# First MLP step interleaved by column block, memory keys and second block's scores later, last norm's vectors loaded after the output weights

## The chip, the cores and the metric

The kernel runs on one core of a Trainium2 chip. The metric is the device time of one execution in microseconds; a kernel's figure is the median of several runs. The engines are PE (TensorE, the matrix products; PEld are its weight loads), ACT (ScalarE), DVE (VectorE), POOL (GpSimd) and SP (SyncE, which here issues almost all transfers). PSUM holds the results of products in banks, SBUF everything else.

## What is computed

The input is x of 256 positions by 1024 channels, with 256 memory rows. Two hybrid layers and one closing block follow, all in float32:

```
hybrid_layer (twice):
    h = rms_norm(x, ln_mix);  z = h @ w_in
    o_nsa, o_gla, o_mem = sparse attention, gated linear attention, cross-attention into mem
    merged = sum over b of sigmoid(gate_b) * (o_b @ w_branch[b])
    x = x + merged @ w_out
    x = x + square(relu(rms_norm(x, ln_mlp) @ w_up)) @ w_down
second block (once):
    z = x @ w_in;  a gated-MLP branch, a convolution branch, a MoBA attention branch (8 heads)
    merged as above, each branch gated
    x = layer_norm(2 ** 0.25 * x + merged @ w_out, ln_g, ln_b)
```

The keys and values of the cross-attention are rms_norm(mem, mem_norm) @ w_kv, with weights of their own in each layer.

## The kernel before

**Products in three parts.** A float32 weight is loaded raw as 128 x 1024 (512 KB, four buffers `raw`, issued by SP, line 457). `split` (lines 435 to 442) makes its high part on ACT (L441), for every sixth weight on POOL (L439), and its low part raw − high on DVE (L442); `hi` and `lo` have four buffers each. Activations are kept as high and low parts as well (`hilo`, lines 526 to 532: the high part on ACT, L531, the low part on DVE, L532). A product is then high times high, high times low and low times high (`mm3`). In the first MLP matrix the high and low activations stand side by side (tile `hx`), so that one product of 512 columns does two of the three parts and one of 256 columns, with the weight's low part, does the third.

**Order of the work.** The order of PE's instructions is written out by hand: the big products are the trunk, and side work is put in between as *chains*, Python generators that emit some instructions and yield a delay. `pump()` (line 138), called in the trunk after one or a few products, emits what is due by a clock that adds up the estimated durations of the products; `need(hh, k)` (line 157) emits chains until the columns k of an activation exist, and `finish(c)` (line 148) empties a chain. The queues of ACT, DVE, POOL and SP are put in order by a planner: by when an instruction could run in its estimate, and in program order among those that could. PSUM has four accumulators (`acc`), three buffers for side work (`psm`) and one more (`pso`).

**First MLP step.** At the end of the attention part of a layer, `out_proj` (line 1176) adds merged @ w_out to X in two halves of the columns; a chain (`start_x`, `x_transposed`, lines 534 to 559) turns X into the columns `hx`, two column blocks per group of four transposes (L192) into one psm buffer. `up_first` (lines 1364 to 1375) computes the first 512 of the 4096 hidden units. It fills four accumulators: for each half of the contraction (`hf`, four blocks k) and each half of the units (`c`), the code takes column block `cb`, in it first the four products with high weights, then the four with low weights, 64 products in all. X's blocks 4 to 7 are transposed while the first half runs. In layer 0 the memory columns for layer 1's keys are also made here: `mem_start(1, mem1[0], 1000.0)` (line 1401, defined at 604) starts a chain of four groups of four transposes of `gate` (where the memory rows were loaded), due 1000 ns after the step's start and 300 ns after each other. Their conversions write two `b8x` tiles. After the step, `mem_kv` (lines 609 and 1404) multiplies them with the key weights. The relu and square of the step's result follow in `up` (line 1328).

**Second block's attention.** `moba` (lines 1520 to 1579) is one chain over four pairs of heads. `scores(pr)` emits eight score products and four bias products into two psm buffers; DVE takes the maxima, ACT the exponentials (L1542), DVE normalizes. The next pair's scores come 3000 ns later, the transposes of the pair (L1550) 6500 ns after that. Meanwhile the trunk multiplies with w_in. The chain is collected at `finish(c_att)` (line 1616).

**Last projection and norm.** In the second block `out_proj` is called with "none": the first half of the columns as usual, the second half (lines 1178 to 1194) from four more weights, with the layer norm (`fin`, lines 1647 to 1670) following each half of the rows. The norm's gain and offset, each spread over 128 partitions (512 KB), are loaded into the buffer `hx`, which has one copy and is free after the last product with `hx`; the loads (L1641, L1642) stand in the program ahead of the output weights, and they are read at L1666 and L1669.

Of the kernel before, what the change touches and what calls it, by code (L numbers as in the profile page):

```python
# [10 lines left out]
F32 = mybir.dt.float32  # L11
# [8 lines left out]
P = 128  # L20
# [78 lines left out]
def block_kernel(ctx, tc, x_in, mem_in, positions, ln_mix, w_in, b_merge, nsa_q_norm, nsa_k_norm,  # L99
# [5 lines left out]
    nc = tc.nc  # L105
# [7 lines left out]
    big = ctx.enter_context(tc.tile_pool(name="big", bufs=1))  # L113
# [24 lines left out]
    def pump():  # L138
        for c in list(chains):
            while not c[2] and c[1] <= clock[0]:  # L140
                advance(c)
# [15 lines left out]
    def need(hh, k):  # L157
        r = ready.get(id(hh))
        while r is not None and r[1][0] <= k:
            nxt = min(chains, key=lambda d: d[1])  # L160
            if nxt[1] > clock[0]:
                clock[0] = nxt[1]
            advance(nxt)
# [78 lines left out]
    def wrap(ap, dims):  # L242
        return bass.AP(tensor=ap.tensor, offset=ap.offset, ap=dims)
# [218 lines left out]
    def units(w2d, r0, nk, cols, paired=None, fine=False):  # L462
        n = sum(c1 - c0 for c0, c1 in cols)
        per = max(1, 1024 // n)
        if paired:
            c0, c1 = cols[0]
            res = []
            for k in range(0, 4, per):
                srcs = [(slice(64 * j, 64 * j + 64), 0, n,
                         w2d[256 * j + 64 * k:256 * j + 64 * (k + per), c0:c1].rearrange("(a d) n -> d a n", d=64))  # L470
                        for j in range(2)]
                h, lo = unit(srcs, per, n)
                res += [(h[:, j, :], lo[:, j, :]) for j in range(per)]
            return res
        res = []
        k = 0
        while k < nk:
            a = min(per, nk - k)
            rs = w2d[r0 + k * P:r0 + (k + a) * P, :]
            srcs = []  # L480
            o = 0
            for c0, c1 in cols:
                srcs.append((slice(0, P), o, o + c1 - c0, rs[:, c0:c1].rearrange("(a p) n -> p a n", p=P)))
                o += c1 - c0
            h, lo = unit(srcs, a, n, fine and k == 0)
            if fine and k == per:
                fine()
            for j in range(a):
                res.append((h[:, j, :], lo[:, j, :]))
            k += a  # L490
        return res
# [112 lines left out]
    def mem_start(l, MEM, lat=0.0):  # L604
        mh, ml = B8("b8x", FR), B8("b8x", FR)
        start_x(MEM, mh, ml, 32 + 8 * l, None, lat)
        return mh, ml
# [568 lines left out]
    def out_proj(w2d, mg, fin, gcol, mid=None):  # L1176
        for h in range(2):
            if gcol == "none" and h == 1:
                ws = units(w2d, 0, 8, [(512, 1024)])
                ts_ = slice(0, P)  # L1180
                ps = ACC()
                for k, (wh, wl) in enumerate(ws):
                    mm3(ps, mg[0][:, k, ts_], mg[1][:, k, ts_], wh, wl, k == 0, k == 7)
                fin(0, 2, ps)
                fin(0, 4, None)
                ts_ = slice(P, 2 * P)
                for q in range(2):
                    qs = slice(256 * q, 256 * q + 256)
                    ps = ACC()
                    for k, (wh, wl) in enumerate(ws):  # L1190
                        mm3(ps[:, 0:256], mg[0][:, k, ts_], mg[1][:, k, ts_], wh[:, qs], wl[:, qs], k == 0, k == 7)
                    fin(1, 2 + q, ps[:, 0:256])
                fin(1, 4, None)
                continue
            ps = tok_major(mg[0], mg[1], w2d, 0, 8, [(512 * h, 512 * h + 512)])
            for tt in range(2):
                fin(tt, h, ps[tt])
            if gcol == "none":
                continue
            if h == 0:  # L1200
                halves = [1]
                hT = HX()
                hc = start_x(X, *hT, gcol, halves, 1500.0)
                if mid is not None:
                    mid()
        if gcol == "none":
            return None
        halves[0] = 2
        return hT[0], hT[1], hc

    def layer(l, hT):
        hh, hl, hc = hT
# [83 lines left out]
        mg = None  # L1296
        for b in (2, 1, 0):
# [7 lines left out]
            else:  # L1305
                oT = o_nsa
                finish(c_nsa)
                mg = (B8("b8x", FR), B8("b8x", FR))
# [11 lines left out]
        mem1 = []  # L1320
# [43 lines left out]
        def up_first():  # L1364
            p2 = [ACC() for _ in range(4)]
            for hf in range(2):
                for c in range(2):
                    ws = units(w_up[l], 512 * hf, 4, [(256 * c, 256 * c + 256)])
                    for cb in range(2):
                        for part in range(2):  # L1370
                            for k in range(4 * hf, 4 * hf + 4):
                                need(hh, k)
                                up_product(p2[2 * c + cb], k, cb, ws[k - 4 * hf][part], part)
                                pump()
            return p2

        def dn(gi):
# [20 lines left out]
                    pump()  # L1398

        if l == 0:  # L1400
            mhl = mem_start(1, mem1[0], 1000.0)
        up(0)
        if l == 0:
            mem_kv(1, *mhl)
# [12 lines left out]
    def layer_2(hT):  # L1417
# [102 lines left out]
        def moba():  # L1520
            UE = {}

            def scores(pr):
                p = [PS(), PS()]
                for q0, k1 in ((0, P), (P, 256)):
                    for j in range(2):
                        rr = slice(64 * j, 64 * j + 64)
                        mm(p[j][:, q0:q0 + k1], CQ[rr, pr, q0:q0 + P], CK_[rr, pr, 0:k1], q0 == 0, False)
                for j in range(2):
                    sl = SLP[:, 2 * pr + j, :]  # L1530
                    mm(p[j][:, 0:P], sl, DM[:, 0:P], False, True)
                    mm(p[j][:, P:384], sl, DM[:, P:384], False, True)
                res = []
                for j in range(2):
                    n = SM([P, 2], "n0")
                    dve.tensor_reduce(n[:, 0:1], p[j][:, 0:P], op=OP.max, axis=AX, negate=True)
                    dve.tensor_reduce(n[:, 1:2], p[j][:, P:384], op=OP.max, axis=AX, negate=True)
                    e = T2("pexp")[:, 0:384]
                    s = SM([P, 2], "s0")
                    cuts = (slice(0, P), slice(P, 384))  # L1540
                    for i, cs in enumerate(cuts):
                        act(e[:, cs], p[j][:, cs], AF.Exp, bias=n[:, i:i + 1], accum_out=s[:, i:i + 1])  # L1542
                    r = SM([P, 2], "r0")
                    dve.reciprocal(r, s)
                    for i, cs in enumerate(cuts):
                        dve.tensor_scalar(e[:, cs], e[:, cs], r[:, i:i + 1], None, op0=OP.mult)
                    res.append(e)
                UE[pr] = res

            def transp(e):  # L1550
                pt = PS()
                for i in range(3):
                    tr(pt[:, i * P:i * P + P], e[:, i * P:i * P + P], IDF)
                pts = T2("pts")[:, 0:384]
                act(pts, pt[:, 0:384], AF.Copy)
                return pts

            scores(0)
            po = None
            for pr in range(4):  # L1560
                a = pr % 2
                if pr + 1 < 4:
                    yield 3000.0
                    scores(pr + 1)
                yield 6500.0
                t = [transp(e) for e in UE.pop(pr)]
                yield 2000.0
                if a == 0:
                    yield from take_po()
                    po = PO()  # L1570
                for kt in range(2):
                    for j in range(2):
                        h = 2 * pr + j
                        o = po[64 * j:64 * j + 64, 256 * a + P * kt:256 * a + 256]
                        mm(o, CVv[kt][:, h * 64:h * 64 + 64], t[j][:, 256 * kt:256 + P * kt], kt == 0, kt == 1)
                if a == 1:
                    act(AT[:, pr - 1:pr + 1], v2(po), AF.Copy)
                    free_po()
            yield 1000.0
# [56 lines left out]
            oT = (ya, yb, yc)[b] if bi == 2 else (ya, None, yc)[b]  # L1636
            M = merge_branch(w_branch_2[0, b], oT, g, M, bi == 2, mg)

        LGT = big.tile([P, 2, 1024], F32, tag="hx", name="LGT", bufs=1)
        LG = LGT  # L1640
        nc.sync.dma_start(LGT[:, 0], wrap(ln_g_2[0], [[0, P], [1, 1024]]))  # L1641
        nc.sync.dma_start(LGT[:, 1], wrap(ln_b_2[0], [[0, P], [1, 1024]]))  # L1642

        alpha = 2.0 ** 0.25
        fst = {}
# [1 line left out]
        def fin(tt, h, ps):  # L1647
# [20 lines left out]
            for q, qs in enumerate(cuts):  # L1668
                dve.scalar_tensor_tensor(X[:, tt, qs], X[:, tt, qs], rs, LG[:, 1, qs], op0=OP.mult, op1=OP.add)  # L1669
                nc.sync.dma_start(out[0, tt * P:(tt + 1) * P, qs], X[:, tt, qs])  # L1670
        out_proj(w_out_2[0], mg, fin, "none")

    hh0, hl0 = HX()
    hT = [hh0, hl0]
# [43 lines left out]
```

## Time and profile before

| | us |
|---|---|
| runs | 1221.73, 1219.28, 1221.53 |
| median | 1221.53 |
| profiled execution | 1223.66 |
| its span | 1221.9 |
| TensorE busy | 1201.4 (98%) |
| VectorE busy | 871.5 (71%) |
| ScalarE busy | 605.1 (50%) |
| GpSimd busy | 199.5 (16%) |

The profile comes from one execution of the program. The span is the time from its first to its last instruction. The mean granted clock of TensorE is 0.994 of full speed. An instruction's row gives its start, its duration and, in brackets, how long the engine stood idle before it and what released it. Rows of the same kind in a sequence are merged, with their count (x4). Matmuls overlap each other, so the distance from one start to the next, not the duration shown, tells what a product costs.

### The profile page before, as it was taken

The numbers are of one execution on the slowest core, as the hardware profiler recorded it, in microseconds if no ns is written. First come the engines' busy times: TensorE is split into PE (matmuls) and PEld (weight loads), VectorE is DVE, ScalarE is ACT, GpSimd is POOL, SyncE is SP. The second block draws the span as 40 slices with busy tenths as digits, with TensorE's granted clock in tenths as the row PEclk, the third lists the DMA queues.
The fourth block names the chain that finished last, engine by engine and source line by source line (L and its number), as shares of the span: only waits on it lengthen the run. The fifth ranks groups of instructions, "written<-read, shape, count | busy, mean of one in ns | idle before, by whom it ended". The sixth has DMA issues, their size and how long they took to land. (4 is left out here: it accounts for less than half of the span.)

```text
span 1221.9 us, 17759 instructions
## 1 busy us (share of the span) xinstructions
PE 1201.4 (98%) x6553; PEld 1004.8 (82%) x6553; DVE 871.5 (71%) x1457; ACT 605.1 (50%) x988; POOL 199.5 (16%) x235
## 2 busy tenths in 40 slices
PE   9999999999999999999999999999999999999997
PEld 6897777888788888888777888888888997998876
DVE  5977978677665656658868867665555799985677
ACT  7557544434645445466645444554554334443351
POOL 2310220120111112200312020121111111000201
PEclk9999999999999999999989999999999999999999
DMA  8567523676566666657613576656666555466662
GB/s 279 178 178 205 157 88 108 191 220 209 156 186 187 193 193 188 181 158 186 202 59 104 171 200 194 187 176 201 183 197 196 180 174 172 132 184 198 176 206 70
DMA packets 138699, 213.91 MB, mean 175 GB/s; under 512 B 12145, under 2 KB 76757, under 8 KB 138612
## 3 DMA queue, kind: packets, MB, share of 16 engines
q1 hardware_dynamic: 137284, 209.19, 57.8%
q0 software_dynamic: 1152, 3.31, 0.9%
q8 instruction: 51, 0.84, 0.3%
q14 instruction: 36, 0.29, 0.1%
q10 hardware_dynamic: 176, 0.27, 0.1%
HBM read 211.86 MB, written 1.05 MB: 174 GB/s over the span
## 5 line engine op out<-in xcount | busy, mean ns | idle before, releaser
L442 DVE TENSOR_TENSOR lo<-raw,hi 128x1024 fp32r<-128x1024 f32 (+1 forms) x369 | 458.6, 1246 | 219.9 <-ACT hi L441 169.4
L441 ACT ACTIVATE hi<-raw 128x1024 fp32r<-128x1024 f32 (+1 forms) x308 | 322.8, 1057 | 344.4 <-PE acc L188 284.5
L188 PE MATMUL acc<-hi,hx 128*128 128x512 f32 (+1 forms) x1024 | 338.3, 395 | 0.0
L188 PEld LDWEIGHTS acc<-hi,hx 128*128 128x128 f32 x1024 | 192.0, 189 | 40.2 <-issue 4.0
L188 PE MATMUL acc<-lo,hx 128*128 128x512 f32 (+1 forms) x512 | 197.3, 385 | 0.0
L439 POOL TENSOR_SCALAR hi<-raw 128x1024 fp32r<-128x1024 f32 x61 | 74.5, 1222 | 611.4 <-PE acc L188 438.5
L188 PE MATMUL acc<-hi,oh 128*128 128x512 f32 x400 | 157.9, 395 | 0.0
L188 PE MATMUL acc<-lo,oh 128*128 128x512 f32 x400 | 155.9, 390 | 0.0
L188 PE MATMUL acc<-hi,ol 128*128 128x512 f32 x400 | 155.8, 390 | 0.0
L188 PE MATMUL acc<-hx,hi 128*128 128x256 f32 (+1 forms) x704 | 137.7, 297 | 1.7 <-DVE hx L532 1.7
L188 PEld LDWEIGHTS acc<-hx,hi 128*128 128x128 f32 x704 | 110.9, 191 | 6.4 <-issue 2.3
L188 PE MATMUL psm<-hx,hi 128*128 128x512 f32 x448 | 111.8, 391 | 0.0
L188 PEld LDWEIGHTS acc<-lo,hx 128*128 128x128 f32 x512 | 96.9, 189 | 16.4
L188 PE MATMUL acc<-hi,b8x 128*128 128x512 f32 (+1 forms) x336 | 106.1, 388 | 1.4 <-ACT b8x L531 0.8
L188 PE MATMUL acc<-hx,lo 128*128 128x256 f32 x384 | 101.7, 284 | 0.3 <-DVE lo L442 0.3
L188 PEld LDWEIGHTS psm<-hx,hi 128*128 128x128 f32 x448 | 81.4, 189 | 15.1
L188 PEld LDWEIGHTS acc<-hi,ol 128*128 128x128 f32 x400 | 75.1, 188 | 15.9
L188 PEld LDWEIGHTS acc<-hi,oh 128*128 128x128 f32 x400 | 75.2, 188 | 14.7
L188 PEld LDWEIGHTS acc<-lo,oh 128*128 128x128 f32 x400 | 75.2, 188 | 14.6
L188 PEld LDWEIGHTS acc<-hi,b8x 128*128 128x128 f32 x336 | 62.3, 189 | 14.3 <-DVE b8x L532 1.5
L188 PEld LDWEIGHTS acc<-hx,lo 128*128 128x128 f32 x384 | 71.1, 191 | 1.5 <-DVE lo L442 0.5
L1351 POOL TENSOR_TENSOR tmp<-gtmp 128x512 f32<-128x512 f32 x32 | 39.1, 1223 | 165.7 <-ACT gtmp L1346 165.7
(359 smaller groups left out, 1464.4 us busy)
## 6 DMA issues: line engine op xcount, KB each, us to landing
raw<-in_w_in SPq DMA_DIRECT2D x160, 512.0 KB
raw<-in_w_up SPq DMA_DIRECT2D x64, 512.0 KB
raw<-in_w_down SPq DMA_DIRECT2D x64, 512.0 KB
raw<-in_w_branch SPq DMA_DIRECT2D x28, 512.0 KB
raw<-in_w_out SPq DMA_DIRECT2D x24, 512.0 KB
raw<-in_cmp_w SPq DMA_DIRECT2D x32, 256.0 KB
raw<-in_mem_w_kv SPq DMA_DIRECT2D x15, 512.0 KB
raw<-in_w_branch SPq DMA_DIRECT2D x16, 256.0 KB
```

The source lines that it names most:

```text
L188: nc.tensor.matmul(o, l, r, start=start, stop=stop, skip_group_check=True)
L439: pool.tensor_scalar(hi, raw, 1.0, 1.0, op0=OP.mult, op1=OP.mult)
L441: act(hi, raw, AF.Copy)
L442: dve.tensor_tensor(lo, raw, f32(hi), op=OP.subtract)
L1351: pool.tensor_tensor(u, r, r, op=OP.mult)
```

## The change

It has three parts. In `up_first`, for every block k the products of both column blocks are issued one after the other, first all of the high weights, then all of the low ones, and chains are emitted after each two products. The start of the memory chain goes from 1000 to 7000 ns. In `moba`, the scores of pair 1 come 6500 ns after those of pair 0 instead of 3000; the other pairs keep 3000. The loads of the last norm's vectors become a function that `out_proj` calls after it has asked for the weights of the second column half, through its parameter `mid`.

```diff
--- before.py
+++ after.py
@@ -1177,6 +1177,7 @@
         for h in range(2):
             if gcol == "none" and h == 1:
                 ws = units(w2d, 0, 8, [(512, 1024)])
+                mid()
                 ts_ = slice(0, P)
                 ps = ACC()
                 for k, (wh, wl) in enumerate(ws):
@@ -1366,12 +1367,12 @@
             for hf in range(2):
                 for c in range(2):
                     ws = units(w_up[l], 512 * hf, 4, [(256 * c, 256 * c + 256)])
-                    for cb in range(2):
-                        for part in range(2):
-                            for k in range(4 * hf, 4 * hf + 4):
-                                need(hh, k)
+                    for part in range(2):
+                        for k in range(4 * hf, 4 * hf + 4):
+                            need(hh, k)
+                            for cb in range(2):
                                 up_product(p2[2 * c + cb], k, cb, ws[k - 4 * hf][part], part)
-                                pump()
+                            pump()
             return p2
 
         def dn(gi):
@@ -1398,7 +1399,7 @@
                     pump()
 
         if l == 0:
-            mhl = mem_start(1, mem1[0], 1000.0)
+            mhl = mem_start(1, mem1[0], 7000.0)
         up(0)
         if l == 0:
             mem_kv(1, *mhl)
@@ -1560,7 +1561,7 @@
             for pr in range(4):
                 a = pr % 2
                 if pr + 1 < 4:
-                    yield 3000.0
+                    yield 6500.0 if pr == 0 else 3000.0
                     scores(pr + 1)
                 yield 6500.0
                 t = [transp(e) for e in UE.pop(pr)]
@@ -1636,10 +1637,11 @@
             oT = (ya, yb, yc)[b] if bi == 2 else (ya, None, yc)[b]
             M = merge_branch(w_branch_2[0, b], oT, g, M, bi == 2, mg)
 
-        LGT = big.tile([P, 2, 1024], F32, tag="hx", name="LGT", bufs=1)
-        LG = LGT
-        nc.sync.dma_start(LGT[:, 0], wrap(ln_g_2[0], [[0, P], [1, 1024]]))
-        nc.sync.dma_start(LGT[:, 1], wrap(ln_b_2[0], [[0, P], [1, 1024]]))
+        LG = big.tile([P, 2, 1024], F32, tag="hx", name="LG", bufs=1)
+
+        def load_lg():
+            nc.sync.dma_start(LG[:, 0], wrap(ln_g_2[0], [[0, P], [1, 1024]]))
+            nc.sync.dma_start(LG[:, 1], wrap(ln_b_2[0], [[0, P], [1, 1024]]))
 
         alpha = 2.0 ** 0.25
         fst = {}
@@ -1668,7 +1670,7 @@
             for q, qs in enumerate(cuts):
                 dve.scalar_tensor_tensor(X[:, tt, qs], X[:, tt, qs], rs, LG[:, 1, qs], op0=OP.mult, op1=OP.add)
                 nc.sync.dma_start(out[0, tt * P:(tt + 1) * P, qs], X[:, tt, qs])
-        out_proj(w_out_2[0], mg, fin, "none")
+        out_proj(w_out_2[0], mg, fin, "none", load_lg)
 
     hh0, hl0 = HX()
     hT = [hh0, hl0]
```

## Rows read from the trace of the kernel before

**Rows 1.** The page's first section: busy us of each engine, share, instructions

```profile
PE 1201.4 (98%) x6553; PEld 1004.8 (82%) x6553; DVE 871.5 (71%) x1457; ACT 605.1 (50%) x988; POOL 199.5 (16%) x235
```

**Rows 2.** Waits of PE: total us, times, longest us

```profile
PE acc L188 <- DVE hx L532: 1.7, 1, 1.7
...
PE acc L188 <- DVE lo L442: 0.5, 2, 0.3
```

**Rows 3.** Timeline of PE, first MLP step, layer 0: start, us, what, [idle before]

```profile
302.07 1.07 PE L188 MATMUL acc<-hx,hi 128*128 128x512 f32 x4
...
306.29 0.63 PE L192 MATMUL psm<-CF,gate 128*128 128x128 f32 x4 [0.32 <-DVE b8x L532]
306.68 0.36 PE L188 MATMUL acc<-hx,lo 128*128 128x256 f32 x1
...
314.12 0.50 PE L188 MATMUL acc<-hx,hi 128*128 128x512 f32 x1 [1.74 <-DVE hx L532]
...
319.14 0.40 PE L188 MATMUL acc<-hi,b8x 128*128 128x512 f32 x1
```

**Rows 4.** Timeline of PE, first MLP step, layer 1

```profile
776.63 1.07 PE L188 MATMUL acc<-hx,hi 128*128 128x512 f32 x4
...
780.90 0.60 PE L192 MATMUL psm<-CF,X 128*128 128x128 f32 x4
...
783.08 1.09 PE L188 MATMUL acc<-hx,hi 128*128 128x512 f32 x4
...
788.70 0.63 PE L188 MATMUL psm<-hx,hi 128*128 128x512 f32 x2
```

**Rows 5.** Stretches: busy PE, PEld, DVE, ACT, POOL; granted clock, DMA share, GB/s

```profile
302.00:320.00 18.00, 15.60 (x94) 12.95 (x93) 12.00 (x21) 10.26 (x20) 1.55 (x2) 1.00 0.43 125
1060.00:1080.00 20.00, 19.74 (x166) 18.64 (x164) 20.00 (x43) 10.81 (x21) 1.65 (x1) 1.00 0.53 150
```

**Rows 6.** Timeline of all engines, first MLP step, layer 0

```profile
311.36 1.05 POOL L439 TENSOR_SCALAR hi<-raw 128x1024 fp32r<-128x1024 f32 x1 [19.70 <-PE acc L188]
...
312.44 1.23 DVE L442 TENSOR_TENSOR lo<-raw,hi 128x1024 fp32r<-128x1024 f32 x1 [1.02 <-POOL hi L439]
```

**Rows 7.** Timeline of PE, second block's scores, pairs 0 and 1

```profile
1015.69 0.93 PE L188 MATMUL psm<-g,g 64*128 64x128 f32 x8
...
1016.81 0.48 PE L188 MATMUL acc<-hi,hx 128*128 128x512 f32 x1
...
1020.42 0.48 PE L188 MATMUL psm<-g,g 64*128 64x128 f32 x2
1022.07 0.92 PE L188 MATMUL psm<-g,g 64*128 64x128 f32 x6 [1.17 <-ACT pexp L1542]
...
1023.18 0.47 PE L188 MATMUL acc<-hi,hx 128*128 128x512 f32 x1
```

**Rows 8.** Timeline of SP's queue at the output weights

```profile
1175.59 3.49 SPq L457 DMA_DIRECT2D raw<-in_w_out  x2
...
1179.64 0.65 SPq L1642 DMA_DIRECT2D LGT<-in_ln_b  x1
1180.39 16.50 SPq L457 DMA_DIRECT2D raw<-in_w_out  x6
```

**Rows 9.** Chain of waits that ended last: start, us, what

```profile
1180.39 8.11 DMA raw<-in_w_out
```

**Rows 10.** Timeline of all engines at the output projection's start

```profile
1188.61 1.06 ACT L441 ACTIVATE hi<-raw 128x1024 fp32r<-128x1024 f32 x1 [3.53 <-DMA raw<-in_w_out]
...
1190.20 0.49 PE L188 MATMUL acc<-hi,b8x 128*128 128x512 f32 x1 [0.77 <-ACT b8x L531]
...
1191.58 0.73 PE L188 MATMUL acc<-hi,b8x 128*128 128x512 f32 x2 [0.65 <-DVE b8x L532]
```

**Rows 11.** Timeline of all engines where the last norm begins

```profile
1210.95 1.41 DVE L1666 SCALAR_TENSOR_TENSOR X<-X,bmv,LGT 128x512 f32<-128x512 f32 x2
```

**Rows 12.** Timeline of SP's queue in layer 1

```profile
670.76 0.26 SPq L1421 DMA_DIRECT2D a<-in_conv_w  x1
```

## The prediction

> **What bounds the kernel now.** I read the page's first section: TensorE (PE) is busy for 98% of the span; its weight loads overlap that, and no other engine is above 71% [rows 1]. A change that leaves the products as they are can therefore only give back PE's waits, which are 2% of the span, some 20 us, spread over many places. The view of waits by engine and line shows which lie at the edited places; two stand in [rows 2], of 1.7 us and 0.5 us in total. The timeline around each place shows the step that waits, and the table of stretches how full the other engines are there. So I price each part by the PE time lost at its place, then ask what keeps the loss alive.
>
> The profiled execution took 1223.66 us (span 1221.9), 2.13 above the median of the runs, 1221.53. I subtract gains from 1223.66 and take 2.13 off at the end. 0.2% is 2.4 us, about what a measurement of this kernel can tell from no change.
>
> **First MLP step, interleaved, with later memory keys.** In layer 0 the step's 64 products run from 302.07 to 319.14, 17.07 us [rows 3]. The same step of layer 1 runs from 776.63 to 788.70, 12.07 us, without a wait [rows 4]. Layer 0 carries the memory keys besides: four more groups of four transposes. At 0.63 us of one [rows 3] they are 2.52, so 5.00 − 2.52 = 2.5 us are lost. The stretch 302 to 320 says the same: PE is busy 15.60 of 18.00, idle 2.40 [rows 5]. Counting a group by its start-to-start cost (306.29 to 306.68, 0.39, [rows 3]) gives 5.00 − 1.56 = 3.4, my upper bound.
>
> The loss is mostly one wait: 1.74 us at 314.12 for the low part of X's columns [rows 3]. The chain behind it: the memory groups come first (due 1 us after the step begins), fill the three psm buffers and queue their conversions on ACT and DVE; X's last two groups go out only after the fourth of them, at 306.29 [rows 3]. The last group's conversion on DVE then stands behind a weight's low part, started at 312.44 after waiting 1.02 for a POOL split that had begun at 311.36 [rows 6].
>
> After the change the memory groups are due 7 us in. X's last two groups, due some 4 us in by the kernel's clock, come ahead of them, at about 306.6 for the last (an estimate from the due times in the code). Layer 1 gives the spacing without the memory: its last group starts at 780.90 and the second half of the contraction at 783.08 [rows 4], that is 6.45 us after the step's start, so at 308.5 here. Interleaving moves the first use of the last column from the fourth to the seventh product of that half, three products of about 0.23 us later: 308.5 + 1.4 = 309.9, or 3.3 us after its transposes. Layer 1 does it in 2.18 + 0.7 = 2.9. So the 1.74 goes. Of the remaining 0.66 of idle I keep a quarter, since four memory groups still follow one another: taken gain 2.3, bounds 0 (the conversion is still late) and 3.4.
>
> What moves and what follows it: the memory chain issues 16 transposes, their ACT and DVE conversions and no DMA, so SP's queue is passed by nothing and its raw buffers keep their order. POOL keeps its splits and squares. Conversions now lie around 310 to 315, where the stretch has DVE at 12.00 and ACT at 10.26 of 18 [rows 5]. The memory key products follow the step at about 316.8 and need the first columns: about 4 us after their groups, which are at 310 to 312.6. They also need two of the four accumulators; those of column half 0 end 16 products (2.8 us) before the step's end in either order, so the ACT copy and DVE add that empty them stay covered. If either cover fails, PE waits there for up to the 2.3 gained. In layer 1 the interleaving removes nothing, since no wait is there: zero. It halves the places where chains may be emitted, one after two products instead of each, which shifts a group by at most 0.25 us: zero, covered by the 0.7 later use.
>
> **Second block scores later.** The first head pair's scores run from 1015.69 to the next product at 1016.81, 1.12 us; the second pair's from 1020.42 to 1023.18, 2.76 us, of which 1.17 is a wait for a psm buffer that ACT's exponentials still read [rows 7]. 3.5 us more delay puts them five emission steps later, at about 1023.8, after the buffer came free at 1022.07. Loss between 1.17 and 2.76 − 1.12 = 1.64; I take 1.3. The later pairs and their transposes shift by 3.4 us, with about two more emission steps of room than that before the chain is collected. Queued behind them on DVE are weights' low parts: DVE is busy 20.00 of 20.00 from 1060 to 1080 [rows 5], and one low part already holds PE up (two such waits in the span, 0.3 us the longest, [rows 2]). Moving work out of the early part into this stretch can cost what it gained. So bounds −0.5 (both of those waits once more) and 1.64; I take 1.3, near the wait itself, because the work only moves: what comes later onto DVE has left it earlier.
>
> **Last norm's vectors.** Now SP issues two raw output weights from 1175.59, the two vectors (at 1179.64 the second), then six more weights from 1180.39 [rows 8]. The first of the six takes 8.11 us in the chain of waits [rows 9]; it shares the engines with the two vectors, 512 KB each like itself. ACT's split of it waits 3.53, the conversion of the merged columns stands behind that split, and PE waits 0.77 and 0.65 [rows 10]: 1.42 us to gain if the vectors leave. They are read first at 1210.95 [rows 11]; behind the last weight's issue (1180.39 + 16.50 = 1196.9, [rows 8]) even 8.11 us of transfer ends by about 1206 with both in line, so no new wait: bounds 0 and 1.42.
>
> Whether they leave is the question. SP's order is not the program's: a filter load of line 1421, which belongs to the second block, was issued at 670.76 in the middle of layer 1 [rows 12], as soon as its buffer was free. The vectors too were ahead of the weights in the program and went after two of them, when hx came free. The third weight has to wait for its own raw buffer, SP has nothing else, and the vectors are ready. Written later they are still the only ready load in that gap. I take **zero** here, by that row.
>
> Sum: 2.3 + 1.3 + 0 = 3.6; 1223.66 − 3.6 = 1220.1 profiled, 1217.9 as a median. Own range, by what I kept of each bound: 1216.9 to 1219.0.
>
> **The rivals.**
> *The vectors do leave.* The third weight is ready by the time SP looks, and takes precedence. For it: the gap is about 1 us wide (1179.64 and 1180.39 follow without a pause, [rows 8]), so the planner's own estimate need only be off by that. Against: [rows 12]. Then 1.4 more: 1216.5. Chance 0.26.
>
> *DVE takes the scores' gain back.* For it: 20.00 of 20.00 and a low part with no slack [rows 2, 5]. Against: the work is moved and not added. 1217.9 + 1.3 = 1219.2. Chance 0.12.
>
> *The first step gains nothing*: X's low part is late again, behind a split on POOL as at 311.36 [rows 6], or the memory columns keep PE at the key products. Against: 3.3 us where layer 1 needs 2.9. 1217.9 + 2.3 = 1220.2. Chance 0.13. With both of these, 1221.5, chance 0.09.
>
> *Slower: the clock of TensorE falls.* Interleaved, the step changes its accumulator at every product, 64 times in each layer, where it now changes after eight. If PE paused at each change, its granted clock could drop from 1.00 [rows 5] (2.4 GHz) to the 1.2 GHz level; the step's 12.07 us [rows 4] would double, 12.1 more in one layer: 1230.0, 24 more with both. It turns the result slower from 6 us on, half of one such stretch at the low level. Against: the second block's scores change accumulators at each product, eight in 0.93 us, no longer for one than elsewhere [rows 7]. Chance 0.09. The Trainium skill, page "TensorE: Matmul & The Clock Gate", section "A second HAM failure mode: psum-queue depth-cycling", tells of a kernel that went round its PSUM banks each iteration, idled between groups and saw its clock oscillate. By that rule this rival would hold; this trace has no long stretch of that kind to confirm it.
>
> **How the numbers follow.** Forecast 0.31, rivals as given. Faster by over 0.2% (below 1219.1): the forecast and the first rival nearly whole, and those parts of the next two in which the vectors leave as well: 0.66. Within 0.2%: 0.25. Slower: 0.09. The range leaves out the clock rival and a little below: down to 1214.8 (the vectors leave and the upper bounds 3.4 and 1.64 hold in good part), up to 1221.4.
>
> **What would show it.** Right: the step of layer 0 in about 14.7 us with no wait for hx over 0.3; the second scores in 1.2 us without a wait for pexp; SP's order at the vectors unchanged, with the weight behind them still landing after some 8 us. Wrong: a wait of over 1 us at the key products or before the second half; DVE-low waits on PE between 1024 and 1085 that sum to over 1 us; the vectors behind the last weight; a granted clock below 1.00 in the two steps.

## The result, and the profile after

The changed kernel takes 1216.03 us (median of 5 runs, 1215.75 to 1217.99), the kernel before in the same comparison 1221.73 (1219.28 to 1227.17). The ratio is 0.9946, interval 0.9930 to 0.9961: faster by 0.4 to 0.7%. The forecast was 1217.9 with a range of 1214.8 to 1221.4. So the sign and the range held; the likeliest value was 1.9 us too high, and the narrower range that the forecast gave for itself, 1216.9 to 1219.0, was missed. The profiled execution took 1215.75 us (span 1214.0, granted clock 0.997).

The first section of the page, as in [rows 1]:

```profile
PE 1195.1 (98%) x6553; PEld 1001.3 (82%) x6553; DVE 869.8 (72%) x1457; ACT 605.0 (50%) x988; POOL 202.1 (17%) x235
```

PE still bounds the kernel. Its waits, from the view that [rows 2] are from (us in total, times, longest us):

```profile
PE acc L188 <- DVE hx L532: 0.7, 1, 0.7
...
PE acc L188 <- DVE lo L442: 0.2, 1, 0.2
```

The waits for pexp and for the merged columns in b8x at the output projection are gone. A wait for hx is still there, 0.7 instead of 1.7 us, and, as the next rows show, it is another one.

**The first MLP step.** Timeline of PE in layer 0, which answers to [rows 3]:

```profile
301.03 1.98 PE L188 MATMUL acc<-hx,hi 128*128 128x512 f32 x8
...
305.62 0.60 PE L192 MATMUL psm<-CF,X 128*128 128x128 f32 x4
...
312.51 0.63 PE L192 MATMUL psm<-CF,gate 128*128 128x128 f32 x4 [0.36 <-DVE b8x L532]
...
315.77 0.40 PE L188 MATMUL acc<-hi,b8x 128*128 128x512 f32 x1
```

X's groups come first, the memory's after them, and the step takes 14.74 us instead of 17.07. The 1.74 us wait is gone. The same in layer 1, which answers to [rows 4]:

```profile
771.67 1.98 PE L188 MATMUL acc<-hx,hi 128*128 128x512 f32 x8
...
776.26 0.60 PE L192 MATMUL psm<-CF,X 128*128 128x128 f32 x4
...
778.11 1.55 PE L188 MATMUL acc<-hx,hi 128*128 128x512 f32 x6
780.40 0.73 PE L188 MATMUL acc<-hx,hi 128*128 128x512 f32 x2 [0.74 <-DVE hx L532]
...
784.72 0.63 PE L188 MATMUL psm<-hx,hi 128*128 128x512 f32 x2
```

This step was free of waits and took 12.07 us. Now it takes 13.05, with a wait of 0.74 for the low part of X's last column. The timeline of all engines shows why:

```profile
777.63 1.06 ACT L441 ACTIVATE hi<-raw 128x1024 fp32r<-128x1024 f32 x1
...
778.58 0.47 ACT L531 ACTIVATE hx<-psm,COL 128x256 fp32r<-128x256 f32 x1
...
778.72 1.23 DVE L442 TENSOR_TENSOR lo<-raw,hi 128x1024 fp32r<-128x1024 f32 x1 [0.44 <-ACT hi L441]
...
779.86 0.48 DVE L532 SCALAR_TENSOR_TENSOR hx<-psm,COL,hx 128x256 fp32r<-128x256 f32 x1
```

A weight's split stands between X's third and fourth conversion: its high part on ACT (777.63), its low part on DVE (778.72). The fourth is done at 780.34, and PE starts the products that need it at 780.40.

**The scores.** Timeline of PE, which answers to [rows 7]:

```profile
1019.85 0.93 PE L188 MATMUL psm<-g,g 64*128 64x128 f32 x8
...
1020.97 0.48 PE L188 MATMUL acc<-hi,hx 128*128 128x512 f32 x1
```

Pair 1 takes 1.12 us, as pair 0 did before, instead of 2.76, and waits for nothing.

**The output weights.** Timeline of SP's queue, which answers to [rows 8]:

```profile
1171.07 0.37 SPq L457 DMA_DIRECT2D raw<-in_w_out  x1
1171.94 0.34 SPq L1643 DMA_DIRECT2D LG<-in_ln_g  x1
1173.37 5.11 SPq L457 DMA_DIRECT2D raw<-in_w_out  x4
1178.54 0.46 SPq L1644 DMA_DIRECT2D LG<-in_ln_b  x1
1181.65 6.23 SPq L457 DMA_DIRECT2D raw<-in_w_out  x3
```

Neither did the vectors stay together in their gap, as forecast, nor did they go behind the weights: the gain went out behind one weight, the offset behind five. And timeline of ACT, which answers to [rows 10]:

```profile
1175.77 1.06 ACT L441 ACTIVATE hi<-raw 128x1024 fp32r<-128x1024 f32 x1 [1.71 <-DMA raw<-in_w_out]
1178.64 1.06 ACT L441 ACTIVATE hi<-raw 128x1024 fp32r<-128x1024 f32 x1 [1.81 <-DMA raw<-in_w_out]
```

The longest wait for a weight is 1.81 us, before 3.53, and the merged columns are converted in time (from 1181.24). PE has no wait there; before it had 0.77 and 0.65 [rows 10]. PE's timeline at that place, which answers to the rows of [rows 10]:

```profile
1183.49 0.40 PE L188 MATMUL acc<-hi,ol 128*128 128x512 f32 x1
1183.72 0.39 PE L188 MATMUL acc<-hi,b8x 128*128 128x512 f32 x1
...
1184.18 0.62 PE L188 MATMUL acc<-hi,b8x 128*128 128x512 f32 x2
```

In the kernel before, the first of these products stands at

```profile
1189.03 0.40 PE L188 MATMUL acc<-hi,ol 128*128 128x512 f32 x1
```

From there to the product that waited second (1191.58, [rows 10]) it took 2.55 us, now, from 1183.49 to 1184.18, 0.69: 1.86 less, though the two idle times add up to 1.42. Products overlap, so the idle time in brackets is shorter than the delay here; the distance between starts tells the loss (below: "by starts").

### The profile page after: what moved, and what is told of

It reads as the page before. It is cut to its first block, busy times and chain, and to the rows that moved or that the text cites. A ratio compares the mean times of both kernels' runs of the same rounds, so it can differ in the third digit from the quotient of the medians.

```text
span 1214.0 us, 17754 instructions
## 1 busy us (share of the span) xinstructions
PE 1195.1 (98%) x6553; PEld 1001.3 (82%) x6553; DVE 869.8 (72%) x1457; ACT 605.0 (50%) x988; POOL 202.1 (17%) x235
```

## The experiments

Runs of one and the same kernel spread over 2 to 8 us, and the kernel before had medians of 1221.7 to 1225.0 in the five comparisons. Most of this spread goes with the run's mean granted clock: of the kernel before, the 13 runs at 0.993 took 1225.5 us on average, the 15 at 0.997 took 1221.2, the 5 at 0.999 took 1219.9; the last section shows where the clock falls. Times are therefore compared as ratios to the kernel before of the same comparison, and effects under 2 us are read from the timelines, where a step repeats within 0.05 us.

### One part undone at a time

**The loop as before** (run twice, the second time beside the changed kernel):

```diff
-                    for part in range(2):
-                        for k in range(4 * hf, 4 * hf + 4):
-                            need(hh, k)
-                            for cb in range(2):
+                    for cb in range(2):
+                        for part in range(2):
+                            for k in range(4 * hf, 4 * hf + 4):
+                                need(hh, k)
                                 up_product(p2[2 * c + cb], k, cb, ws[k - 4 * hf][part], part)
-                            pump()
+                                pump()
```

> The changed kernel with the loop of the first MLP step as before (column block outermost); memory keys at 7000, scores and vectors as changed. Theory: the late memory chain alone frees layer 0's step, and the interleaving is what made layer 1's step longer (13.05 us, with a wait of 0.74, where it took 12.07). Then layer 0's step takes 14.3 to 15.2 us (14.74 in the changed kernel, 17.07 before), layer 1's 12.1 without a wait, and the median is 0.5 to 1.5 below the changed kernel's 1216.0: 1214.5 to 1215.5. Rival: the interleaving carries the gain of layer 0 by its later first use; then that step takes over 16 us and the median is 1216.5 to 1217.5, layer 1's step being 12.1 all the same.

Measured: 1215.57 us, ratio 0.9941 [0.9924, 0.9959]. Layer 0's step takes 14.19 us, layer 1's 12.06 without a wait. The theory holds and the rival falls: with the memory late, the interleaving gives nothing in layer 0 and costs about 0.5 there and 1.0 in layer 1. The repetition:

> The changed kernel once more, beside the next three on the same chip. Expected: 0.993 to 0.996 of the kernel before; layer 1's step 13.05 us with the wait of 0.74, layer 0's 14.7, no wait over 0.2 in the second block. If the wait of layer 1 is not there again, it was an accident of one execution and not the change's.

> The changed kernel with the loop as before (column block outermost) once more. Theory: the interleaving costs 0.98 in layer 1 and 0.5 in layer 0, so this is 1.0 to 1.7 us below a_after in the same comparison. Rival: the two differ by under 0.5; the timeline's difference is made up elsewhere.

Measured: changed kernel 1216.93, ratio 0.9951 [0.9934, 0.9968]; old loop 1216.35, ratio 0.9952 [0.9937, 0.9967]. The profiled spans are 1214.3 and 1212.2. The steps repeat: 14.71 and 13.05 (wait 0.74) against 14.21 and 12.05. PE's timeline of the old loop in both layers (start and end of the two steps):

```profile
300.47 1.07 PE L188 MATMUL acc<-hx,hi 128*128 128x512 f32 x4
...
314.68 0.40 PE L188 MATMUL acc<-hi,b8x 128*128 128x512 f32 x1
...
770.60 1.07 PE L188 MATMUL acc<-hx,hi 128*128 128x512 f32 x4
...
782.64 0.63 PE L188 MATMUL psm<-hx,hi 128*128 128x512 f32 x2
```

The 1.5 us of the two steps are there in the timelines; the two medians differ by 0.6 with overlapping intervals and do not prove it alone.

**The memory chain at 1000 again:**

```diff
-            mhl = mem_start(1, mem1[0], 7000.0)
+            mhl = mem_start(1, mem1[0], 1000.0)
```

> The changed kernel with the memory chain due 1000 ns after the step's start again; the interleaving stays. Theory: the four memory groups ahead of X's last two are the cause of the lost 2.3 us, and the interleaving does not make up for them: layer 0's step 16.5 to 17.5 us, with a wait for hx of over 1 us, median 1217.8 to 1218.8. Rival: the later first use of the last column (three products, 0.7 us) is enough: step under 15.2 us, median 1216 to 1216.5.

Measured: 1219.27, ratio 0.9969 [0.9956, 0.9982]. PE's timeline of the step:

```profile
307.37 0.63 PE L192 MATMUL psm<-CF,X 128*128 128x128 f32 x4 [0.60 <-DVE b8x L532]
...
308.79 0.63 PE L192 MATMUL psm<-CF,gate 128*128 128x128 f32 x4 [0.79 <-DVE b8x L532]
```

The step takes 15.66 us (302.77 to 318.43), between theory and rival. The wait for hx is gone, so the later first use does help when the memory is early; but the transposes now wait for their psm buffers (0.60 and 0.79). Of the 17.07 us, interleaving alone takes 1.41, the late memory alone 2.88, both together 2.33.

**Pair 1's scores at 3000 again:**

```diff
-                    yield 6500.0 if pr == 0 else 3000.0
+                    yield 3000.0
```

> The changed kernel with pair 1's scores 3000 ns after pair 0's again. Theory: the wait for the exponentials comes back (1.1 to 1.3 us) and pair 1's scores take 2.7 us instead of 1.1; nothing of it is given back later, so the median is 1.5 to 2 above the changed kernel's: 1217.5 to 1218. Rival: VectorE, full from 1024 to 1085, had taken a part back; then PE's waits for low parts in that stretch are smaller here than in the changed kernel (0.0 there) and the median is within 0.7 of 1216.0. The planner also puts the first vector of the last norm behind two more weights here; with weights in time in both orders that changes nothing.

Measured: 1217.77, ratio 0.9964 [0.9952, 0.9977]. PE's timeline:

```profile
1017.81 0.92 PE L188 MATMUL psm<-g,g 64*128 64x128 f32 x6 [1.15 <-ACT pexp L1543]
```

Pair 1's scores take 2.75 us again, and the wait of 0.24 for a low part at 1062 is back as well. Theory holds: 1.63 + 0.24, nothing given back. The vectors left behind the third and the fifth weight here, again without a wait of PE.

**The vectors ahead again:**

```diff
+        nc.sync.dma_start(LG[:, 0], wrap(ln_g_2[0], [[0, P], [1, 1024]]))
+        nc.sync.dma_start(LG[:, 1], wrap(ln_b_2[0], [[0, P], [1, 1024]]))
+
         def load_lg():
-            nc.sync.dma_start(LG[:, 0], wrap(ln_g_2[0], [[0, P], [1, 1024]]))
-            nc.sync.dma_start(LG[:, 1], wrap(ln_b_2[0], [[0, P], [1, 1024]]))
+            pass
```

> The changed kernel with the two vectors of the last norm asked for ahead of the output weights again; the planner puts both behind the first weight. Theory: 1 MB ahead of the second and third weight makes them late (over 6 us each or together), ScalarE stands in their split with the merged columns' conversion queued behind it, and PE waits 1.3 to 2.2 us at the start of the output projection: median 1217.3 to 1218.2. Rival: one vector more or less ahead is not what decides, the gain there came from the other order of work on ScalarE; then PE waits under 0.4 us there and the median is within 0.5 of 1216.0.

Measured: 1219.00, ratio 0.9967 [0.9953, 0.9981]. The chain of waits that ended last (start, us, what):

```profile
1176.54 7.88 DMA raw<-in_w_out
...
1184.52 1.07 ACT hi L441
...
1186.84 0.61 DVE b8x L532
```

Both vectors leave behind the first weight here. A weight takes 7.88 us again, its split and low part stand ahead of the merged columns' conversion, and PE waits 0.65 at 1187.49. The mechanism is the theory's; the wait is half of what it said. By starts the loss is larger: at 1170 this trace's products come 2.1 us later than the changed kernel's, at the end 3.8, so 1.7 us are lost in between. Why it is less than in the kernel before was not tried; there two weights went ahead of the vectors, here one.

### Why layer 1 became slower

In the change two things differ from the old loop: a unit's high weights are in use for 8 products instead of 12, so their buffer comes free earlier; and chains are emitted after two products instead of one, so X's groups go out later. Three kernels separate these. The first goes further with the interleaving:

```diff
-                    for part in range(2):
-                        for k in range(4 * hf, 4 * hf + 4):
-                            need(hh, k)
+                    for k in range(4 * hf, 4 * hf + 4):
+                        need(hh, k)
+                        for part in range(2):
```

> The changed kernel with the interleaving taken further: for every block k, high weights for both column blocks, then low ones. The accumulators alternate as in the change, but a unit's high weights are in use until the 14th of its 16 products instead of the 8th (before: the 12th), and the last of X's columns is first used at the 13th product of its half instead of the 7th. Theory: in the change the high buffer comes free early, so the next weight's split goes ahead of X's last conversion on ScalarE and VectorE; here it does not, and layer 1's step takes 12.06 us without a wait, layer 0's 14.2 to 14.7, the median 1.0 to 1.6 below a_after. Rival: the change of accumulator at every product is what costs; then layer 1's step is 12.8 or more again.

Measured: 1216.85, ratio 0.9952 [0.9936, 0.9967]; layer 0's step 14.10, layer 1's 12.82 with a wait of 0.54; the median is the changed kernel's (1216.93) and not 1.0 to 1.6 below it. My theory of the early release fell: the buffer comes free late, and the split still gets ahead. The timeline of all engines in layer 1:

```profile
778.58 1.23 DVE L442 TENSOR_TENSOR lo<-raw,hi 128x1024 fp32r<-128x1024 f32 x1 [0.57 <-ACT hi L441]
...
779.73 0.48 DVE L532 SCALAR_TENSOR_TENSOR hx<-psm,COL,hx 128x256 fp32r<-128x256 f32 x1
```

The second is the change with chains emitted after every product:

```diff
                             for cb in range(2):
                                 up_product(p2[2 * c + cb], k, cb, ws[k - 4 * hf][part], part)
-                            pump()
+                                pump()
```

> The changed kernel's interleaving with chains emitted after every product instead of every second. X's groups go out one product earlier. In the queues, layer 0 has X's four conversions in a row again and then the weight's low part; in layer 1 the low part still stands ahead of X's last conversion on VectorE. Theory (that place in the queue is what costs): layer 1 keeps a wait for hx of 0.2 to 0.7, a little under the changed kernel's 0.74, and layer 0 has none. Rival (only the lateness of X's groups costs): no wait for hx in either layer, layer 1's step 12.06.

Measured: 1216.94, ratio 0.9944 [0.9929, 0.9959]; layer 0's step 14.40 without a wait for hx, layer 1's 12.83 with a wait of 0.51. DVE's timeline in layer 0, first of the changed kernel:

```profile
307.92 1.23 DVE L442 TENSOR_TENSOR lo<-raw,hi 128x1024 fp32r<-128x1024 f32 x1 [0.27 <-POOL hi L439]
309.06 0.48 DVE L532 SCALAR_TENSOR_TENSOR hx<-psm,COL,hx 128x256 fp32r<-128x256 f32 x1
```

Then of this run:

```profile
307.92 1.51 DVE L532 SCALAR_TENSOR_TENSOR hx<-psm,COL,hx 128x256 fp32r<-128x256 f32 x3 [0.42 <-ACT hx L531]
309.35 1.21 DVE L442 TENSOR_TENSOR lo<-raw,hi 128x1024 fp32r<-128x1024 f32 x1
```

In the changed kernel a low part stands ahead of X's last conversion in layer 0 too, and PE starts the products that need it at 309.59, 0.72 us after the group of transposes before them (308.87), where such a group otherwise takes 0.35; so the interleaving costs something here in the same way. In this run the conversions stand in a row, and the step is 0.34 shorter. In layer 1 the low part is still ahead, and the wait stays. This is what the theory said. The third has both, the order of the first and the emission of the second:

> The order of e6_k_outer with chains emitted after every product. Late release of a unit's high weights and early groups together: in both layers X's four conversions stand in a row in both queues, ahead of the next weight. Theory: layer 1's step 12.05 to 12.1 us without a wait though the accumulator changes at every product, layer 0's 14.1 to 14.3, median 1 to 1.6 below the changed kernel, like the old loop. Rival (alternating accumulators costs): layer 1's step 12.4 or more.

Measured: 1216.35, ratio 0.9942 [0.9929, 0.9955]; layer 0's step 14.40 (0.1 above the range expected), layer 1's 12.02 without a wait. DVE's timeline in layer 1, and the stretch (busy PE, PEld, DVE, ACT, POOL, granted clock, DMA share, GB/s):

```profile
776.44 2.05 DVE L532 SCALAR_TENSOR_TENSOR hx<-psm,COL,hx 128x256 fp32r<-128x256 f32 x4
779.01 1.23 DVE L442 TENSOR_TENSOR lo<-raw,hi 128x1024 fp32r<-128x1024 f32 x1 [0.52 <-ACT hi L441]
```

```profile
771.50:783.50 12.00, 12.00 (x74) 10.55 (x73) 8.42 (x12) 7.02 (x12) 2.02 (x3) 1.00 0.59 181
```

X's four conversions stand in a row, and the wait is gone. So in layer 1 two things mattered, how often chains are emitted and the order of the loop: either of them as in the change leaves a wait of half a microsecond, both together 0.74, and in each of these cases a weight's split stands ahead of X's last conversion. That the order of the loop acts through the early free buffer is argued and not shown, for it also sets where the last column is first used, at the 13th product in the third kernel; the old loop has no wait with the 4th, so that is not needed for it. Which estimate of the planner tips the order was not tried. The alternation of accumulators itself costs nothing: 64 products, with another accumulator at every product, in 12.02 us at a granted clock of 1.00.

### Two doses

**Memory at 5000 instead of 7000**, with the old loop:

> The old loop with the memory chain due at 5000 instead of 7000 ns: its first group then comes right behind X's last one, still in the first half of the contraction. Theory: all that counts is that X's groups go first; layer 0's step 14.2 to 14.6 us, median within 0.5 of a_old_loop. Rival: the memory conversions take ScalarE and VectorE from X's last column also when they come just behind it; then a wait for hx of over 0.5 returns and the step takes over 15 us.

Measured: 1215.53, ratio 0.9943 [0.9925, 0.9962]; the step 14.48 us, without a wait for hx, with one of 0.42 for a psm buffer of the memory groups. So what counts is that X's groups go first; 2 us of distance are worth 0.3.

**Pair 1's scores at 5000 instead of 6500**, with the old loop:

> The old loop in the first MLP step, memory keys at 7000, and pair 1's scores 5000 ns after pair 0's (before 3000, changed 6500): three emission steps later than before instead of five. Theory: the buffer of the exponentials is free 6.4 us after pair 0's scores began; this puts pair 1 at about 6.8, so its wait is under 0.2 and its scores take 1.1 to 1.3 us; the small wait for a low part on VectorE (0.24 to 0.26 at 3000, none at 6500) may come back. Rival: the buffers come free later than that when the scores come later; then a wait of over 0.5 stays.

Measured: 1218.56, ratio 0.9960 [0.9946, 0.9973]. The scores wait for nothing (1019.50, 1.12 us). But PE's timeline shows the wait that the prediction had as a rival:

```profile
1049.48 0.39 PE L188 MATMUL acc<-hx,lo 128*128 128x256 f32 x1 [1.47 <-DVE lo L442]
```

An expected 0.24 to 0.26 became 1.47. Counted by starts against the old loop's trace, PE loses 2.3 us around this wait, much of the 2.2 to 3.0 by which the median is above the old loop's. DVE is busy 20.00 of 20.00 us from 1040 to 1060 here as in the changed kernel, so no idle time of DVE is the difference. The low part that PE waits for (DVE, 1048.22 to 1049.43) comes right behind score work of DVE (L1547, to 1048.30); at 6500 no low part is waited for there.

### The vectors behind the weights

The last run puts the vectors into a buffer that comes free only in the last merge, with the old loop otherwise:

```diff
-        LG = big.tile([P, 2, 1024], F32, tag="hx", name="LG", bufs=1)
+        LG = B8("gate", shape=(2, 1024))
```

> The old loop in the first MLP step with the rest as changed, and the last norm's vectors in the buffer of the merge gates, which comes free only in the last merge, instead of hx. So the planner really issues them behind the output weights (one behind the seventh, one behind the eighth); every other queue is as in a_old_loop. Theory: with the vectors gone from between the weights, ScalarE's waits for the second and third output weight (2.0 and 2.0 us in a_old_loop) shrink to under 1, VectorE's merge work comes earlier, PE has no wait over 0.15 from 1160 on (the changed kernel's order had 0, 0.14 and, in e9_pump_each, 1.2 there), the vectors land before 1195 and nothing waits for them at 1201: median 0 to 0.8 below a_old_loop's two (1215.6 and 1216.4), so 1215.0 to 1216.2. Rival: the vectors now meet the last two weights or come too late for the norm; then a wait of over 0.5 appears after 1185 and the median is above 1216.5.

Measured: 1215.10 (1213.96 to 1218.58), ratio 0.9933 [0.9912, 0.9955], the lowest median, but its interval overlaps those of the changed kernel and of the old loop. By starts its trace lags the old loop's by 0.80 us at 1166 and by 0.79 at the end: from the merge on, the vectors' place gave nothing beyond the old loop, and that the median is lower is not shown to come from the edit. SP's queue:

```profile
1169.78 12.63 SPq L457 DMA_DIRECT2D raw<-in_w_out  x7
1185.63 0.34 SPq L1643 DMA_DIRECT2D gate<-in_ln_g  x1
1187.62 0.37 SPq L457 DMA_DIRECT2D raw<-in_w_out  x1
1188.04 0.46 SPq L1644 DMA_DIRECT2D gate<-in_ln_b  x1
```

Now the loads do go behind the weights, PE has no wait above 0.13 there, and the norm starts at 1202.05 without one. One expectation failed: a weight is still waited for by ACT for 2.98 us, hidden from PE. In the order of the change the margin is thinner: in the run with chains after every product, whose SP queue is the change's, a weight's split began 1.1 us later than in the change's execution (1176.83, not 1175.77) and PE waited 1.20 us for the merge at 1181.09. One such case in the executions profiled is no rate.

## Why the prediction was right and where it was wrong

**Layer 0's step: right in size, for half the reason.** Taken 2.3, measured 2.33. X's groups went ahead of the memory's, as argued. But the prediction credited the later first use by the interleaving as well; with the memory late it is worth nothing: the old loop gains 2.88, so the interleaving took 0.5 back.

**Layer 1's step: wrong.** The step "In layer 1 the interleaving removes nothing, since no wait is there: zero" and "zero, covered by the 0.7 later use" failed: it cost 0.98. X's last group went out 4.59 us after the step's start instead of 4.27 [rows 4], a shift of 0.32 where 0.25 was allowed for. What failed was the assumption that the queues of ACT and DVE keep their order. They were planned anew, a weight's split (1.06 us on ACT, 1.23 on DVE) got between X's conversions, and that outweighed the 0.7.

**Scores: right, a little low.** Taken 1.3; measured 1.65 at the place, the upper bound, and 0.24 more because a low part later on was no longer late. The lower bound of −0.5 was not reached; the 5000 run shows that it was no empty fear, with a wait of 1.47.

**Vectors: wrong.** The step "Written later they are still the only ready load in that gap. I take zero here" was half right for the first vector, which went out as soon as hx was free (1171.94), and wrong for the second, which lost its place to four weights. The sign that the forecast named, SP's order unchanged, did not show. The term was 0 and became 1.42, the upper bound, in idle time; by starts 1.86 at that place and 1.8 from the last merge to the end, so that the upper bound too was too small: it added up idle times. Half a megabyte in the gap instead of a whole one was enough. The first rival, the vectors leaving, was the nearer case in its time, 1216.5.

**The clock rival fell**: the granted clock was 1.00 in the changed kernel's step in both layers (301 to 316 and 771.5 to 785), and in the run with alternating accumulators and no wait the engine did not pause between them (12.00 busy of 12.00). The Trainium skill's page "TensorE: Matmul & The Clock Gate", section "A second HAM failure mode: psum-queue depth-cycling", tells of a kernel that cycled through PSUM banks, idled briefly between groups of products and saw its clock oscillate. The traces here have the cycling without the idling, and the clock stayed.

**The sum.** By the steps, with idle times for the last two: 2.33 − 0.98 + 1.65 + 0.24 + 1.42 = 4.7 us, against 3.6 taken. The two errors, −0.98 and +1.42, partly cancelled; that the time came out inside the range is in part luck. Matched product by product, PE's starts in the two traces draw apart by 2.3 in layer 0's step, −1.0 in layer 1's, 1.7 at the scores, 0.5 at the low part and 1.8 from the last merge to the end: 5.3 us. The medians differ by 5.7 (interval 4.8 to 8.6 from the ratio). Runs at the same granted clock, 0.997, agree with that: 1221.2 for the kernel before (mean of 15) and 1215.8 for the changed one (mean of 3), 5.4 apart. So the edited places make up the difference of the medians, within what the runs can tell.

## What to carry to other kernels

Where a planner orders the queues, changing the order of one engine's work reorders the others: price the conversions that share a queue with weights again, also in a stretch that has no wait now. Here a load that was written later moved only when its buffer came free later or another load was ready before it; in the one run that chose the buffer for it, both loads went where they were meant to. Price a wait by the starts of the products around it and not by the idle time alone. When two edits aim at one wait, run each alone: here the smaller one brought nothing beside the larger and cost 1.5 us in the two layers.

## What was not expected of the hardware

At two places that no edit touches, TensorE's granted clock falls for a few microseconds in some executions and not in others. The stretches 160 to 165 and 630 to 635 (columns as in the stretch above), kernel before:

```profile
160.00:165.00 5.00, 5.00 (x20) 3.55 (x20) 3.24 (x14) 2.65 (x5) 1.42 (x4) 0.67 0.00 0
630.00:635.00 5.00, 5.00 (x23) 3.69 (x24) 2.82 (x12) 1.15 (x4) 0.00 (x0) 0.59 0.02 3
```

Changed kernel:

```profile
160.00:165.00 5.00, 5.00 (x27) 3.67 (x26) 4.42 (x17) 3.05 (x5) 2.33 (x5) 1.00 0.00 0
630.00:635.00 5.00, 5.00 (x23) 3.71 (x20) 3.26 (x15) 2.59 (x4) 2.01 (x4) 0.78 0.00 0
```

A mean below 1.00 is a stretch of which a part ran at the lower of the two levels, 1.2 of 2.4 GHz. Without any wait, the same products take longer, first in the kernel before, then in the changed one:

```profile
160.16 1.55 PE L188 MATMUL pso<-pts,n 128*64 128x256 f32 x8
```

```profile
160.35 0.87 PE L188 MATMUL pso<-pts,n 128*64 128x256 f32 x8
```

The profiled execution of before has both falls, that of the changed kernel only a shorter one at the second place; of the other twelve, six have the first alone, five the second alone, and the one with the vectors ahead has both. What a fall costs can be read from the old loop's two executions, which are one kernel: one fell at the first place, the other at the second; their starts draw 1.5 us apart at the first and come together again by 1.5 at the second, and both spans are 1212.2. Between the traces of before and after, PE's starts draw 1.3 us apart at the first place and 1.6 at the second; with the 5.3 of the edited places, less 0.2 that the changed kernel loses at its start, that makes about the 7.9 us by which the two spans differ.

Both places have the same work ahead of them: the only two sequences in the kernel of 32 products of 16 columns each (3.64 us from 155.23 in the kernel before, 4.03 from 627.82). In all 14 profiled executions these falls begin within 1.3 us of the start of the last of these products, and every execution falls behind at least one of the two sequences. The products there are the same in every kernel; why one execution falls behind the first and another behind the second stays open, and no run changed these products.
